# Sums of h stored in the v stage, two gate/up splits moved, and another product order in a block's first step

## The chip, the cores and the metric

One core of a Trainium2 chip runs one program. TensorE (PE) multiplies, VectorE (DVE), ScalarE (ACT) and GpSimd (POOL) work element by element, and SyncE (SP) issues nearly all the DMAs. The metric is the device time of one execution in microseconds, and the figure is the median of several runs.

## The reference

One layer of a flow-matching backbone runs on 128 context tokens and 512 latent tokens with a model width of 2048. Everything is float32.

```python
sh1, sc1, g1, sh2, sc2, g2 = adaln(cond, w_ada, b_ada)        # silu(cond) @ w_ada, split in 6
h = rms_norm(x, norm1_g) * (1 + sc1) + sh1
q, k, v, u = split(h @ w_in, 4)                               # 2048 x 4096; q and k normed per head
attn = neighbourhood_attention(q, k, v, cache_k, cache_v, rpb)  # context tokens: dense attention
pool = (centred window means of u, minus u) @ w_pool * pool_scale
x = x + g1 * (concat(rms_norm(attn), rms_norm(pool)) @ w_out)
h = rms_norm(x, norm2_g) * (1 + sc2) + sh2
x = x + g2 * ((silu(h @ w_gate) * (h @ w_up)) @ w_down)       # width 5632
```

The outputs are x for both kinds of tokens and the keys and values of the context tokens.

## The kernel before

All 640 tokens are one operand. Activations lie transposed: a tile has 128 features in the partitions and 640 tokens in the free dimension.

**The large products.** Every float32 operand is split in a high and a low float32r part (hi and lo), and a product takes three matmuls: hi by hi, lo by hi, hi by lo (L400, L401, L402 in `products`). On top of that each pair of weight tiles by a pair of activation tiles goes through a seven-product scheme. A *step* is one pair of 128-row weight tiles: seven products, 21 matmuls of 128x320 or 128x322. A *block* is the steps that add up in the same seven PSUM banks (eight steps in the input, output, gate and up stages, four or five in the down stage). At the end of a block `combine` reads the banks: ACT copies the first (L408), and seven sums on DVE follow (L407). The third and the fourth sum after it read the bank of product 3 and, for the second time, that of product 2.

**Work around a step.** `fetch` loads a weight pair four steps ahead (tile wf, three buffers), `sums` forms the weight sums three steps ahead on POOL (L327), `x_hi` and `x_lo` split them two steps ahead on ACT (L336) and DVE (L342). Other work is hung on later steps with `at`.

**The v stage** comes first. For each of 8 pairs of feature tiles (a *v block*), `turn` transposes the normed x, ACT and DVE write the modulated h (hhi by L244, the float32 h in two reused tiles c by L245), and POOL forms hlo (L246). Then 10 groups of six 128x512 matmuls give v (L163 to L165), added up by DVE (L682). SP loads w_in for it (raw, L148) and, during the first half, the shift and scale part of w_ada (araw, L196, three buffers); the transposes and the adaLN products for the next v blocks are in between.

**The first input block** needs sums of h for the seven-product scheme. `plan_h` puts hi and lo together again into tile f (L628), forms the three sums (`y_sum`, L361), and splits them into h's own tile and t (ACT L636, L637; DVE or POOL L644). A planner (`issue`) writes this order out from durations and due times, together with the first eight steps, and it picks DVE or POOL for each operation.

**The gate and up stage** has 22 pairs of blocks, a gate block and an up block. After the up block of a pair, its end work hangs on the next steps by the tables FF_TIGHT, FF_WIDE and FF_LAST, in half steps: scale by rho (L1654), add the shift (L1659), multiply by the gate (L1642), sums (L1669), and four splits (`f_split`, ACT L1679 and DVE L1680) that are stored to DRAM (L1683, L1684). FF_WIDE holds for pairs 4 to 20. The down stage loads these operands back (L1703).

The instructions of every engine stand in the order that the program writes from the first input block on; in the v stage PE's order is written, and a scheduler sets that of the others.

Of the kernel before, what the change touches and what calls it, by code (L numbers as in the profile page):

```python
# [9 lines left out]
F32 = mybir.dt.float32  # L10
# [8 lines left out]
P = 128  # L19
# [30 lines left out]
def tile_hybrid_step(  # L50
# [51 lines left out]
    def c_tile(i):  # L102
        return cp.tile([P, 2 * HX], F32, tag=f"c{i}", name=f"c{i}", bufs=1)
# [9 lines left out]
    c_s = dram.tile([P, NKT, 32], F32, name="c_s")  # L113
    x_s = dram.tile([NKT, P, TOK], F32, name="x_s")
    h2_s = dram.tile([NKT, P, TOK], F32, name="h2_s")

    yh_s = dram.tile([NPAIR, P, 7, HB], F32, name="yh_s")
    yl_s = dram.tile([NPAIR, P, 7, HB], F32, name="yl_s")
# [107 lines left out]
    def turn(kt, eng=nc.gpsimd):  # L226


        by_column = lambda v: v.rearrange("p (c r) -> p c r", r=ROWS)
        ps_s = pp.tile([P, 512], F32, tag="tp", name="ps_s")  # L230
        ps_p = pp.tile([P, P], F32, tag="tq", name="ps_p")
        for t in range(4):
            nc.tensor.transpose(ps_s[:, t * P : (t + 1) * P], xn[t][:, kt * P : (kt + 1) * P], ident)
        nc.tensor.transpose(ps_p, xn[4][:, kt * P : (kt + 1) * P], ident)
        h = c_tile(kt % 2)[:, 0:TOK]
        hi, lo = h_hi[kt], h_lo[kt]
        for s in range(2):
            g, b = gs[1][:, kt, s : s + 1], sh[1][:, kt, s : s + 1]
            if s == 0:
                src = ps_s.rearrange("p (r c) -> p c r", r=ROWS)  # L240
                to = [by_column(v[:, 0:SMP]) for v in (hi, h)]
            else:
                src, to = ps_p, [v[:, SMP:TOK] for v in (hi, h)]
            nc.scalar.activation(to[0], src, AF.Identity, bias=b, scale=g)  # L244
            nc.vector.tensor_scalar(to[1], src, g, b, op0=ALU.mult, op1=ALU.add)  # L245
        eng.tensor_tensor(lo, h, hi.bitcast(F32), op=ALU.subtract)  # L246

    starts = [(k, 2) for k in range(0, NKT, 2)]
    done = [0]
# [37 lines left out]


    PRODUCTS = ((6, 6), (1, 1), (0, 0), (2, 2), (3, 5), (5, 3), (4, 4))
    EARLY_FIRST = (0, 4, 6, 1, 2, 3, 5)  # L290
    GROUPS = ((0, 4), (4, 9), (9, 13), (13, 18), (18, 22))
    YB = 7
# [104 lines left out]
    def products(ps, x, y, first, last, order):  # L397
        for n in order:
            b, (i, j) = ps[n], PRODUCTS[n]
            mm(b, lhsT=x[0][:, i, :], rhs=y[j][0], start=first, stop=False)  # L400
            mm(b, lhsT=x[0][:, i, :], rhs=y[j][1], start=False, stop=False)  # L401
            mm(b, lhsT=x[1][:, i, :], rhs=y[j][0], start=False, stop=last)  # L402
# [11 lines left out]
        add(c[2], c[2], p4)  # L414
        add(c[0], c[0], p2)

    def step(ps, y, first, out, order=range(7), last=False):

        s = now[0]
        now[0] = s + 1  # L420
        fetch(s + 4)
        sums(s + 3)
        if out is None:
            prepare(s + 2)
        for fn, args in jobs.pop((s, 0), ()):
            fn(*args)
        products(ps, xs.pop(s), y, first, last or out is not None, order)
        if out is not None:
            combine(ps, out)
            prepare(s + 2)  # L430
        for fn, args in jobs.pop((s, 1), ()):
            fn(*args)
# [186 lines left out]
    t_tiles = {}  # L619

    def plan_h(i, key):
        g, s = place("f"), place("f")
        y = lambda: (four(s, HB), four(g, HB))

        def join(e, j):
            d = g.tile[:, 2 * j * HB : 2 * j * HB + TOK]
            kt = 2 * i + j
            E[e].tensor_tensor(d, h_hi[kt].bitcast(F32), h_lo[kt].bitcast(F32), op=ALU.add)  # L628

        got = take(key, g, s)  # L630
        joined = [on("DVE Pool", key, TOK, lambda e, j=j: join(e, j), (got,), (g,)) for j in range(2)]
        summed = plan_y_sums(key, y, g, s, HB, joined)

        def hi(e):
            t_tiles[i] = [tl.tile([P, 3, HB], F32R, name=f"t{n}{i}") for n in ("hi", "lo")]
            nc.scalar.copy(h_hi[2 * i + 1][:, HB:TOK], four(s, HB)[:, 0, :])  # L636
            nc.scalar.copy(t_tiles[i][0], four(s, HB)[:, 1:4, :])  # L637

        def lo(e, part):
            if part == 0:  # L640
                out, src, minus = h_lo[2 * i + 1][:, HB:TOK], four(s, HB)[:, 0, :], h_hi[2 * i + 1][:, HB:TOK]
            else:
                out, src, minus = t_tiles[i][1], four(s, HB)[:, 1:4, :], t_tiles[i][0]
            E[e].tensor_tensor(out, src, minus.bitcast(F32), op=ALU.subtract)  # L644

        his = on("ACT", key, 4 * HB, hi, summed, (s,))
        return [
            on("DVE Pool", key, n, lambda e, part=part: lo(e, part), (his,), (s,)) for part, n in ((0, HB), (1, 3 * HB))
        ]

    def h_operand(i):
        out = []
        for h, t in zip((h_hi, h_lo), t_tiles[i]):
            even, odd = h[2 * i], h[2 * i + 1]
            out.append([odd[:, HB:TOK], t[:, 0, :], t[:, 1, :], t[:, 2, :], even[:, 0:HB], even[:, HB:TOK], odd[:, 0:HB]])
        return list(zip(*out))


# [2 lines left out]
    for b, (k0, n) in enumerate(starts):  # L661
        more = b + 1 < len(starts)
        if not more:
            close(sp_cm)
            gu = ctx.enter_context(tc.tile_pool(name="gu", bufs=1, side="right", reuse_waits="tile"))
            fp_cm, fp = pool("fp", side="right")
            for s in range(3):
                fetch(s)
        group = 0
        for vb in range(2):  # L670
            raw = load_k(w_in, k0, n, 2 * AW + vb * 512, 512, wp.tile([P, 1024], F32, tag="raw", name="raw", bufs=3)[:, 0 : n * 512])
            ws = [split(raw[:, i * 512 : i * 512 + 512]) for i in range(n)]
            for t in range(NT):
                tk = slice(t * P, (t + 1) * P)
                ps = pp.tile([P, 512], F32, tag="g", name="g", bufs=4)
                for i in range(n):
                    mm3(ps, h_hi[k0 + i][:, tk], h_lo[k0 + i][:, tk], *ws[i], i == 0, i == n - 1)
                dst = vacc[t][vb]
                if b == 0:
                    nc.scalar.copy(dst, ps)  # L680
                else:
                    nc.vector.tensor_tensor(dst, ps, dst, op=ALU.add)  # L682
                next(stream, None)
                if more and group == 5:
                    ada_until(b + 2)
                if more and 5 <= group < 5 + starts[b + 1][1]:
                    turn(starts[b + 1][0] + group - 5)
                group += 1
            if not more:
                store_v(vb)  # L690
# [1024 lines left out]
    ada_gen = None  # L1715

    FF_TIGHT = (0, 1, 2, 4, 6, 7, 18, 20)
    FF_WIDE = (2, 4, 6, 8, 10, 12, 18, 20)
    FF_LAST = (2, 3, 4, 8, 16, 18, 10, 12)
    WIDE = 4  # L1720

# [258 lines left out]
```

## Time and profile before

| | |
|---|---|
| three runs | 2805.04, 2805.74, 2812.82 us; median 2805.74 us |
| profiled execution | 2810.24 us, span 2808.4 us, mean granted clock 0.972 |
| busy share of the span | PE 93%, POOL 70%, DVE 67%, ACT 39% |
| v stage | from the start to 206.05 us |
| input blocks | 206.05 us to about 585 us, the first of them to 263.07 us |
| gate and up stage | about 1032 us to 2209.5 us |

PE's ends are modelled and its matmuls overlap, so its busy share says little about its pace; the pace is read from the starts of the matmuls and from the number of them in a stretch. A step is 21 matmuls. Windows are named by their first and last microsecond from the start of the span.

### The profile page before, as it was taken

What the parts mean: (1) busy time and instruction counts of PE and PEld (TensorE: products, weight loads), DVE (VectorE), ACT (ScalarE), POOL (GpSimd) and SP (SyncE); (2) the same over time, 40 slices, a digit from 0 to 9 for tenths busy, and PEclk for the clock granted to TensorE, in tenths of its full rate; (3) what the DMA queues carried; (4) which work ended last, traced back from release to release, by engine and by line L of the source; (5) the groups of instructions that cost most, each with busy time, mean ns of one, the idle gap of its engine ahead of it and who ended that gap; (6) DMA issues with size and microseconds to landing.
All of it is one profiled execution on the core that took longest, in us unless ns stands there. A gap on an engine that the chain in (4) does not pass through costs nothing.

```text
span 2808.4 us, 46345 instructions
## 1 busy us (share of the span) xinstructions
PE 2622.1 (93%) x16936; PEld 2429.6 (87%) x16936; DVE 1891.1 (67%) x2566; ACT 1088.7 (39%) x1605; POOL 1968.2 (70%) x2264
## 2 busy tenths in 40 slices
PE   5997999988769968998999999999999899999998
PEld 2577888877669968998999999999999889999997
DVE  2478433457875597665787776777867667787776
ACT  3233222246633434443444444444444323333333
POOL 2367565667678876675788877887778656887874
PEclk9998999989989988999999999999999999999999
DMA  9922777677335443655344343343443775365353
GB/s 324 322 88 68 258 261 269 236 211 220 95 123 194 156 146 124 218 169 160 116 135 130 116 142 123 122 142 117 135 130 116 264 242 202 122 220 191 114 166 104
DMA packets 367222, 476.69 MB, mean 170 GB/s; under 512 B 22544, under 2 KB 286224, under 8 KB 366352
## 3 DMA queue, kind: packets, MB, share of 16 engines
q1 hardware_dynamic: 363824, 468.87, 51.2%
q10 hardware_dynamic: 3168, 4.85, 0.6%
q8 instruction: 133, 2.18, 0.3%
q14 instruction: 97, 0.79, 0.1%
HBM read 389.09 MB, written 84.54 MB: 169 GB/s over the span
## 4 chain that ended last, share of the span: by engine, by line
PE 34%; DVE 11%; POOL 7%; DMA 7%; issue 4%; ACT 3%; SPq 0%; ACTq 0%; DVEq 0%; POOLq 0%
PE pp L402 11%; PE pp L400 11%; PE pp L401 11%; POOL wf L327 6%; DVE xlo L342 3%; DVE c L407 2%; ACT xhi L336 2%; DMA wf<-in_w_up_dram 2%; DMA wf<-in_w_gate_dram 2%; DMA wf<-in_w_down_dram 2%; DMA ylo<-yl_s 1%; DVE cx L407 1%; DVE c L1680 1%; DMA araw<-in_w_ada_dram 1%; DVE cx L1680 0%
## 5 line engine op out<-in xcount | busy, mean ns | idle before, releaser
L327 POOL TENSOR_TENSOR wf<-wf 128x128 f32<-128x128 f32 (+1 forms) x2007 | 1642.7, 825 | 574.1 <-DMA wf<-in_w_up_dram 112.9
L400 PE MATMUL pp<-yhi,xhi 128*128 128x322 f32 (+1 forms) x4072 | 1282.9, 315 | 29.5 <-DVE c L407 8.9
L402 PE MATMUL pp<-yhi,xlo 128*128 128x322 f32 (+1 forms) x4072 | 1278.3, 314 | 17.1 <-DVE xlo L342 13.9
L401 PE MATMUL pp<-ylo,xhi 128*128 128x322 f32 (+1 forms) x4072 | 1269.6, 312 | 18.5 <-DVE ylo L381 8.4
L342 DVE TENSOR_TENSOR xlo<-wf,xhi 128x896 fp32r<-128x896 f32 x678 | 809.4, 1202 | 667.9 <-ACT xhi L336 648.6
L336 ACT CAST xhi<-wf 128x896 fp32r<-128x896 f32 x688 | 648.1, 943 | 1241.3 <-POOL wf L327 1091.5
L400 PEld LDWEIGHTS pp<-yhi,xhi 128*128 128x128 f32 x4072 | 775.5, 190 | 60.9 <-DVE c L407 15.4
L402 PEld LDWEIGHTS pp<-yhi,xlo 128*128 128x128 f32 x4072 | 775.2, 190 | 30.6 <-DVE xlo L342 25.8
L401 PEld LDWEIGHTS pp<-ylo,xhi 128*128 128x128 f32 x4072 | 775.5, 190 | 20.7 <-DVE ylo L381 9.3
L407 DVE TENSOR_TENSOR c<-c,pp 128x320 f32<-128x320 f32 (+1 forms) x581 | 253.9, 484 | 44.9 <-ACT c L408 29.2
L400 PE MATMUL pp<-hhi,xhi 128*128 128x320 f32 x384 | 124.7, 325 | 3.1 <-DVE v L682 3.1
L402 PE MATMUL pp<-hhi,xlo 128*128 128x320 f32 x384 | 121.1, 315 | 0.4 <-DVE xlo L342 0.4
L401 PE MATMUL pp<-hlo,xhi 128*128 128x320 f32 x384 | 121.1, 315 | 0.0
L401 PE MATMUL pp<-tlo,xhi 128*128 128x320 f32 x288 | 92.5, 321 | 16.5 <-DVE tlo L644 16.5
L159 POOL TENSOR_TENSOR wlo<-raw,whi 128x512 fp32r<-128x512 f32 x32 | 41.9, 1330 | 81.7 <-ACT whi L158 79.9
L400 PEld LDWEIGHTS pp<-hhi,xhi 128*128 128x128 f32 x384 | 74.0, 193 | 21.9 <-issue 15.1
L402 PE MATMUL pp<-thi,xlo 128*128 128x320 f32 x288 | 91.5, 318 | 0.0
L400 PE MATMUL pp<-thi,xhi 128*128 128x320 f32 x288 | 91.4, 317 | 0.1
L682 DVE TENSOR_TENSOR v<-g,v 128x512 f32<-128x512 f32 x70 | 48.0, 688 | 47.5 <-PE g L165 47.5
L402 PEld LDWEIGHTS pp<-hhi,xlo 128*128 128x128 f32 x384 | 74.0, 193 | 0.7 <-DVE xlo L342 0.7
L401 PEld LDWEIGHTS pp<-hlo,xhi 128*128 128x128 f32 x384 | 74.2, 193 | 0.0
L401 PEld LDWEIGHTS pp<-tlo,xhi 128*128 128x128 f32 x288 | 56.0, 194 | 18.6 <-DVE tlo L644 18.6
(248 smaller groups left out, 2663.4 us busy)
## 6 DMA issues: line engine op xcount, KB each, us to landing
araw<-in_w_ada_dram SPq DMA_DIRECT2D x60, 1024.0 KB, 6.8
wf<-in_w_gate_dram SPq DMA_DIRECT2D x176, 256.0 KB, 2.8
wf<-in_w_up_dram SPq DMA_DIRECT2D x176, 256.0 KB, 3.0
wf<-in_w_down_dram SPq DMA_DIRECT2D x176, 256.0 KB, 3.0
araw<-in_w_ada_dram SPq DMA_DIRECT2D x64, 512.0 KB, 6.6
wf<-in_w_in_dram SPq DMA_DIRECT2D x96, 256.0 KB, 4.1
yh_s<-yh SPq DMA_DIRECT2D x66, 320.0 KB, 3.7
wf<-in_w_out_dram SPq DMA_DIRECT2D x64, 256.0 KB, 2.7
```

The lines of the kernel that those rows point to most:

```text
L159: nc.gpsimd.tensor_tensor(lo, raw, hi.bitcast(F32), op=ALU.subtract)
L327: tt = lambda o, a, b, op: eng.tensor_tensor(o, a, b, op=op)
L336: nc.scalar.copy(hi, raws[s][:, 0:7, :])
L342: eng.tensor_tensor(lo, f[:, 0:7, :], hi.bitcast(F32), op=ALU.subtract)
L400: mm(b, lhsT=x[0][:, i, :], rhs=y[j][0], start=first, stop=False)
L401: mm(b, lhsT=x[0][:, i, :], rhs=y[j][1], start=False, stop=False)
L402: mm(b, lhsT=x[1][:, i, :], rhs=y[j][0], start=False, stop=last)
L407: add = lambda o, a, b: nc.vector.tensor_tensor(o, a, b, op=ALU.add)
L682: nc.vector.tensor_tensor(dst, ps, dst, op=ALU.add)
L1680: nc.vector.tensor_tensor(v, v, hi.bitcast(F32), op=ALU.subtract)
```

## The change

Three edits, and the lines of the file move down by up to 15.

1. In each v block DVE overwrites the two float32 tiles of h with the sums that the scheme needs (`t_sums`, four subtractions of 128x320), and SP stores both tiles to a new DRAM tensor t_s (`t_store`, two DMAs of 320 KB). `plan_h` no longer joins and sums: one DMA of 640 KB loads the four quarters into f. The order of the sums within f differs, and `h_operand` follows it.
2. A block's first step runs its products in the order 0, 1, 3, 2, 4, 5, 6 (FREE_FIRST).
3. FF_WIDE moves the second split of the sums from half step 12 to 22, and the two splits of the product from 18 and 20 to 24 and 26. The entries are in the order scale, shift, times, sums, split of sums 0 and 1, split of the product 0 and 1; here the sums' first split stays at 10.

```diff
+    t_s = dram.tile([NKP, P, 2, TOK], F32, name="t_s")
...
+    h_now = [None, None]
+    def t_sums():
+        (y21, y22), (y11, y12) = ((v[:, 0:HB], v[:, HB:TOK]) for v in h_now)
+        for o, a, b in ((y11, y12, y11), (y12, y22, y12), (y22, y22, y11), (y21, y21, y22)):
+            nc.vector.tensor_tensor(o, a, b, op=ALU.subtract)
+    def t_store(i):
+        for q in range(2):
+            nc.sync.dma_start(t_s[i][:, 1 - q, :], h_now[q])
...
+    FREE_FIRST = (0, 1, 3, 2, 4, 5, 6)
...
-        products(ps, xs.pop(s), y, first, last or out is not None, order)
+        products(ps, xs.pop(s), y, first, last or out is not None, order or (FREE_FIRST if first else range(7)))
...
     def plan_h(i, key):
-        g, s = place("f"), place("f")
-        y = lambda: (four(s, HB), four(g, HB))
-        def join(e, j):
-            d = g.tile[:, 2 * j * HB : 2 * j * HB + TOK]
-            kt = 2 * i + j
-            E[e].tensor_tensor(d, h_hi[kt].bitcast(F32), h_lo[kt].bitcast(F32), op=ALU.add)
-        got = take(key, g, s)
-        joined = [on("DVE Pool", key, TOK, lambda e, j=j: join(e, j), (got,), (g,)) for j in range(2)]
-        summed = plan_y_sums(key, y, g, s, HB, joined)
+        s = place("f")
+        got = op("none", 0.0, key - 6, lambda: None, taken, (s,))
+        taken[:] = [got]
+        loaded = dma(key - 6, 655, lambda: [(s.tile[:, 0 : 4 * HB], t_s[i].rearrange("p a n -> p (a n)"))], (got,), (s,))
+        summed = [loaded]
...
+                if group == 1:
+                    t_sums()
+                if group == 3:
+                    t_store(b)
...
-    FF_WIDE = (2, 4, 6, 8, 10, 12, 18, 20)
+    FF_WIDE = (2, 4, 6, 8, 10, 22, 24, 26)
```

**SP in the v stage.** Before, from the last loads of w_ada (araw) on:

```order
L196 DMA araw<-in_w_ada_dram 128x4x256 x8
L148 DMA raw<-in_w_in_dram 128x2x512
L196 DMA araw<-in_w_ada_dram 128x4x256 x6
L148 DMA raw<-in_w_in_dram 128x2x512 x9
L321 DMA wf<-in_w_in_dram 128x2x256 x3
```

The same place now, c_826 and c_854 being the two tiles of h of v block 3:

```order
L197 DMA araw<-in_w_ada_dram 128x4x256 x6
L260 DMA t_s<-c_612 128x640
L260 DMA t_s<-c_640 128x640
L197 DMA araw<-in_w_ada_dram 128x4x256 x2
L149 DMA raw<-in_w_in_dram 128x2x512
L197 DMA araw<-in_w_ada_dram 128x4x256 x8
L149 DMA raw<-in_w_in_dram 128x2x512
L197 DMA araw<-in_w_ada_dram 128x4x256 x6
L260 DMA t_s<-c_826 128x640
L260 DMA t_s<-c_854 128x640
L149 DMA raw<-in_w_in_dram 128x2x512 x5
```

The stores of v blocks 0, 1 and 2 stand in front of loads of w_ada; those of block 3 and later do not. At the end of the v stage the loads of f stand so, v_155 being the last tile of v:

```order
L293 DMA v_s<-v_153 128x512
L293 DMA v_s<-v_155 128x512
L294 DMA out_dram<-v_155 128x512
L528 DMA f_1624<-t_s 128x1280
L528 DMA f_1625<-t_s 128x1280
L528 DMA f_1626<-t_s 128x1280
L336 DMA wf<-in_w_in_dram 128x2x256
```

The load for the first step (f_1616) is issued four stores earlier in the same queue; those for the later steps stand behind the last store of v.

**DVE in the first input block.** Before, a stretch in its middle:

```order
L628 TENSOR_TENSOR f_1770<-hhi_119,hlo_135 128x640
L628 TENSOR_TENSOR f_1770<-hhi_120,hlo_136 128x640
L644 TENSOR_TENSOR hlo_132<-f_1708,hhi_116 128x320
L644 TENSOR_TENSOR tlo_1746<-f_1708,thi_1745 128x960
L342 TENSOR_TENSOR xlo<-wf,xhi 128x896
L361 TENSOR_TENSOR f_1789<-f_1770 128x2x320
L628 TENSOR_TENSOR f_1821<-hhi_121,hlo_137 128x640
L361 TENSOR_TENSOR f_1789<-f_1770,f_1789 128x320
```

Now, the same place (here L653 is the split, L342 a weight sum and L357 xlo):

```order
L653 TENSOR_TENSOR hlo_129<-f_1625,hhi_113 128x320
L342 TENSOR_TENSOR wf<-wf 128x128 x2
L342 TENSOR_TENSOR wf<-wf 128x256
L653 TENSOR_TENSOR tlo_1700<-f_1626,thi_1699 128x960
L653 TENSOR_TENSOR hlo_133<-f_1660,hhi_117 128x320
L357 TENSOR_TENSOR xlo<-wf,xhi 128x896
```

The joins and the sums of f are gone, and only splits, weight sums and xlo are left; POOL's rows lose the same two kinds.

**DVE in the gate and up stage**, at the end of a gate block. Before, with cx_12756 and cx_12757 the sums of the pair before and c the gate's result:

```order
L342 TENSOR_TENSOR xlo<-wf,xhi 128x896
L1680 TENSOR_TENSOR cx_12756<-cx_12756,yh 128x2x320
L342 TENSOR_TENSOR xlo<-wf,xhi 128x896
L1680 TENSOR_TENSOR cx_12757<-cx_12757,yh 128x2x320
L407 TENSOR_TENSOR c_13313<-c_13312,pp 128x322
```

The same place now:

```order
L357 TENSOR_TENSOR xlo<-wf,xhi 128x896
L1693 TENSOR_TENSOR cx_12762<-cx_12762,yh 128x2x320
L357 TENSOR_TENSOR xlo<-wf,xhi 128x896
L422 TENSOR_TENSOR c_13319<-c_13318,pp 128x322
L422 TENSOR_TENSOR c_13318<-c_13319,pp 128x322
```

The second split no longer stands between the last xlo and the first sum of `combine`; it and the other two now follow the scaling by rho of the gate's result, one a step.

## Rows read from the trace of the kernel before

**Rows 1.** Windows: us; busy of PE, PEld, DVE, ACT, POOL; PEclk; DMA; GB/s.

```profile
69.17:123.72 54.55, 52.17 (x289) 27.50 (x285) 23.05 (x43) 11.69 (x21) 17.48 (x14) 1.00 1.06 344
145.00:190.00 45.00, 44.18 (x207) 35.81 (x206) 26.79 (x43) 13.41 (x24) 24.41 (x19) 1.00 0.20 64
...
206.05:263.07 57.02, 36.84 (x170) 33.94 (x169) 56.61 (x52) 16.45 (x22) 46.02 (x35) 0.77 0.18 59
263.07:288.16 25.09, 25.09 (x169) 25.09 (x169) 11.60 (x15) 7.89 (x9) 11.48 (x18) 0.98 0.58 190
```

**Rows 2.** Group of DVE, 145 to 190 us: busy, mean ns, idle before.

```profile
L682 DVE TENSOR_TENSOR v<-g,v 128x512 f32<-128x512 f32 x30 | 20.7, 689 | 14.6 <-PE g L165 14.6
```

**Rows 3.** Wait of PE, 190 to 263.1 us: total, times, longest.

```profile
PE pp L401 <- DVE tlo L644: 16.5, 7, 3.9
```

**Rows 4.** Groups of DVE in the first input block.

```profile
L628 DVE TENSOR_TENSOR f<-hhi,hlo 128x640 f32<-128x640 f32 x8 | 9.9, 1254 | 0.0
...
L361 DVE TENSOR_TENSOR f<-f,f 128x320 f32<-128x320 f32 x4 | 5.4, 1359 | 0.0
...
L361 DVE TENSOR_TENSOR f<-f 128x640 f32<-128x640 f32 x3 | 3.1, 1043 | 0.0
```

**Rows 5.** Groups of POOL in the same stretch.

```profile
L361 POOL TENSOR_TENSOR f<-f,f 128x320 f32<-128x320 f32 x10 | 13.8, 1380 | 5.9 <-DVE f L361 5.7
...
L628 POOL TENSOR_TENSOR f<-hhi,hlo 128x640 f32<-128x640 f32 x4 | 8.1, 2013 | 1.1 <-DVE tlo L644 1.1
L361 POOL TENSOR_TENSOR f<-f 128x640 f32<-128x640 f32 x4 | 8.0, 2002 | 2.1 <-DVE tlo L644 1.6 <-DVE f L361 0.5
```

**Rows 6.** Timeline of DVE in the first input block: start, duration.

```profile
211.68 1.15 DVE L644 TENSOR_TENSOR tlo<-f,thi 128x960 fp32r<-128x960 f32 x1
...
225.72 2.50 DVE L644 TENSOR_TENSOR tlo<-f,thi 128x960 fp32r<-128x960 f32 x1
...
230.99 0.48 DVE L361 TENSOR_TENSOR f<-f,f 128x320 f32<-128x320 f32 x1
```

**Rows 7.** DMA issues: count, KB each, median us from issue to landing.

```profile
araw<-in_w_ada_dram SPq DMA_DIRECT2D x33, 512.0 KB, 6.6
...
yh_s<-yh SPq DMA_DIRECT2D x66, 320.0 KB, 3.7
```

**Rows 8.** Timeline of SP's DMA issues at the v stage's end.

```profile
210.20 0.48 SPq L280 DMA_DIRECT2D out_dram<-v  x1
```

**Rows 9.** Windows of the gate and up stage.

```profile
1593.58:1618.45 24.87, 24.87 (x170) 24.87 (x169) 19.69 (x22) 10.49 (x18) 20.38 (x23) 1.00 0.32 92
1618.45:1644.78 26.33, 25.65 (x170) 24.91 (x169) 18.18 (x24) 12.07 (x18) 21.40 (x27) 1.00 0.53 167
1340.15:2209.50 869.35, 860.28 (x5714) 846.13 (x5712) 640.64 (x745) 381.92 (x577) 690.08 (x811) 1.00 0.43 134
1365.04:1371.60 6.56, 6.56 (x44) 6.12 (x43) 6.46 (x10) 2.52 (x3) 3.48 (x5) 1.00 0.56 186
...
2181.62:2189.20 7.58, 7.05 (x43) 6.17 (x43) 7.38 (x12) 2.52 (x3) 4.04 (x6) 1.00 0.65 210
```

**Rows 10.** Timeline of DVE at the end of gate block 7.

```profile
1463.53 1.35 DVE L342 TENSOR_TENSOR xlo<-wf,xhi 128x896 fp32r<-128x896 f32 x1
1464.80 1.35 DVE L1680 TENSOR_TENSOR c<-c,yh 128x640 f32<-128x640 f32 x1
1466.08 3.20 DVE L407 TENSOR_TENSOR cx<-cx,pp 128x322 f32<-128x322 f32 x7
```

**Rows 11.** Timeline of PE in the first step of up block 7.

```profile
1466.61 0.41 PE L400 MATMUL pp<-yhi,xhi 128*128 128x322 f32 x1 [0.30 <-DVE cx L407]
...
1467.60 0.41 PE L400 MATMUL pp<-yhi,xhi 128*128 128x322 f32 x1 [0.28 <-DVE cx L407]
```

**Rows 12.** Timeline of DVE there: the fourth sum of `combine`.

```profile
1467.58 0.49 DVE L407 TENSOR_TENSOR cx<-cx,pp 128x322 f32<-128x322 f32 x1
```

**Rows 13.** Window from the last up block into the down stage.

```profile
2188.00:2224.00 36.00, 31.69 (x200) 29.32 (x198) 18.98 (x22) 13.61 (x24) 23.27 (x30) 0.99 0.96 349
```

More of the change, by code (lines that the diff above doesn't have):

```diff
@@ L235, in turn @@
         h = c_tile(kt % 2)[:, 0:TOK]
+        h_now[kt % 2] = h
         hi, lo = h_hi[kt], h_lo[kt]
@@ L415, in combine, with step @@
         add(c[0], c[0], p2)
-    def step(ps, y, first, out, order=range(7), last=False):
+    def step(ps, y, first, out, order=None, last=False):
         s = now[0]
@@ L654, in h_operand @@
             even, odd = h[2 * i], h[2 * i + 1]
-            out.append([odd[:, HB:TOK], t[:, 0, :], t[:, 1, :], t[:, 2, :], even[:, 0:HB], even[:, HB:TOK], odd[:, 0:HB]])
+            out.append([odd[:, HB:TOK], t[:, 2, :], t[:, 0, :], t[:, 1, :], even[:, 0:HB], even[:, HB:TOK], odd[:, 0:HB]])
         return list(zip(*out))
```

## The prediction

> **What bounds the kernel now.** I read the windows by stage first, then PE's waits in the stage that stands out, then the groups and timelines of the engines that it waits for. The profiled execution took 2810.24 us; the median of the runs is 2805.74 us, 4.5 us lower, so I make the sum against 2810.24 and take the difference off the median.
>
> Nearly everywhere PE sets the pace: an input block takes 25.09 us for its eight steps when nothing disturbs it [rows 1], a gate block 24.87 us [rows 9], 3.11 us a step and 0.148 us a matmul. Three places are slower. (a) In the first half of the v stage DMA is full: 1.06 of its time at 344 GB/s over 54.55 us, while PE is busy 52.17 us and DVE 23.05 [rows 1]; that is two v blocks, 27.3 us each. In the second half DMA idles (0.20), PE is full, and DVE has 18 of 45 us free; 30 additions of v are in them, ten a block, so a block takes 15 us and a group 1.5 us [rows 1, 2]. (b) The first input block takes 57.02 us for eight steps. DVE is busy 56.61 us of them and POOL 46.02; PE waits 16.5 us for tlo, seven times, and the granted clock is 0.77 there against 0.98 in the next block [rows 1, 3]. So DVE with POOL bounds it. (c) The 17 gate and 17 up blocks of pairs 5 to 21 take 869.35 us; 34 blocks of 24.87 would be 845.6, so 23.8 us are lost [rows 9]. I took the first two steps of each of the 17 up blocks as a window: first and last are 6.56 and 7.58 us [rows 9], together they are 122.8 us, where a quarter of a quiet block is 6.22 and 17 of them 105.7. So 17.1 of the 23.8 us lie there. Rows 10 and 11 show why: on DVE an xlo, a split, and only then, at 1466.08, the first sum of `combine`; PE's second product starts at 1466.61, its third at 1467.60, each behind a sum that frees its bank.
>
> **Part 1, the first input block.** Removed on DVE: 9.9 + 5.4 + 3.1 = 18.4 us of joins and sums [rows 4]; on POOL 13.8 + 8.1 + 8.0 = 29.9 [rows 5]. Of 56.61 + 46.02 = 102.6 us of work 54.3 are left, 27.2 on each engine if shared evenly, a little over PE's own 25.09. To it comes a start: the load for the first step is early, but the next three stand behind the last store of v, issued at 210.20 to 210.68 [rows 8], 4.6 us into the block; a 320 KB store lands after 3.7 us and a 512 KB load in a full queue after 6.6 [rows 7], so the second operand of 640 KB is there 8 to 11 us into the block, and its ACT and DVE split after that, while the first step keeps PE only 3 us. Half of that gap is caught up while the engines work ahead: 4 us. I take 27.2 + 4 = 31.2 us, 25.8 saved. Bounds: not under 25.09 (32 saved), not over 57.02 (nothing saved).
>
> **Part 1, the v stage.** Added: 32 subtractions of 128x320 on DVE and 16 stores of 320 KB. In the second half a subtraction of 0.48 us [rows 6], four a block, 1.9 us, goes into 18 free of 45 us, nearly three blocks: nothing. In front of them in DVE's queue is the wait for POOL's hlo, and behind them are the additions of v; those have four PSUM banks to wait in, so PE does not see 1 or 2 us. In the first half the cover is gone, since DMA is full. The stores of v blocks 0, 1 and 2 stand in front of loads of w_ada: 3 x 0.655 MB = 1.97 MB, at 344 GB/s 5.7 us [rows 1]. Those of block 3 come behind the last such load. SP waits at a store until the subtractions are done, and the loads of w_ada behind it wait too; in block 0 the transposes come right before, in blocks 1 and 2 half a block earlier, so I count no wait. I take +5.7. Bounds: 0 if PE, which idles only 2.4 of 54.55 us [rows 1], is what bounds the stage after all; +11.5 if SP waits the length of a block's four subtractions, 1.9 us, in front of the loads in each of three blocks.
>
> A store must land before the next `turn` writes the same tile. The sums are done with the end of the transposes' work, half a v block before the next transposes: 7.5 us in the second half, 13 us in the first [rows 1, 2]. Landing takes 3.7 to 6.6 us [rows 7]. So it fits, by 3 us or more in the second half, where DMA is idle and 3.7 us hold.
>
> **Shared ports.** A split of 128x960 on DVE took 1.15 us beside an idle POOL and 2.50 us beside a POOL sum [rows 6]. The Trainium skill (SBUF — State Buffer, Who interferes with whom) says that a DVE instruction with two SBUF inputs and a GpSimd instruction that reads SBUF lock each other out for the whole instruction; the two rows agree. The subtractions are such instructions, in a stage where PE waits for POOL's splits of w_in, so the rule speaks against this part. With the rows' price the worst is 32 x 0.48 = 15.4 us. I count nothing, because POOL is busy 24.41 of 45 and 17.48 of 54.55 us there [rows 1], and keep 15.4 as a rival.
>
> **Part 2, the order of a first step.** The third product already starts at 1467.60, when the fourth sum, which reads product 2 for the last time, has run for 0.02 us [rows 11, 12]. So before the change the third product writes the bank that the third sum frees; the pool hands out banks as they come free. With product 3 in third place it will get the same bank at the same time: 0, in all stages. Bounds: if the banks were fixed it would be worth the length of a sum, 3.20/7 = 0.46 us [rows 10], in the 17 up blocks, 7.8 us either way.
>
> **Part 3, the splits.** The second split stands between xlo and the first sum and takes 1.28 us to the next start [rows 10]. Without it the sums start at 1464.80, and PE's second product, due at about 1466.15, 0.46 us earlier than it started [rows 11], finds its bank free. Over the 17 up blocks a head start of 1.28 us leaves 1.5 of the 17.1 us. The moved splits fall in steps 4 to 6 of the up block, where DVE has little but an xlo of at most 1.35 us in 3.11 us and each split adds at most 1.35; a slip of 1.1 us in total is allowed: 17.1 − 1.5 − 1.1 = 14.5 saved. Bounds: 17.1, and 0 if the wait only moves. ACT's casts and SP's stores move with them; SP waits for the split behind a weight load that is due a step later anyway. For pair 20 they move into the stretch where the down operands are loaded: DMA is 0.96 busy there at 349 GB/s [rows 13]. 0.655 MB of stores more are in it, 1.9 us. The other 6.7 us of (c) stay.
>
> **The sum.** −25.8 + 5.7 − 14.5 + 1.9 = −32.7: 2810.24 − 32.7 = 2777.5 for the profiled execution, 2805.74 − 32.7 = 2773.0 for the median.
>
> **Rivals.**
> - The first block gets a new bound: the loads of f come one after another behind the stores of v, or four buffers of f are too few, and it takes 45 us. For it: issue to landing is 3.7 to 6.6 us, longer than a step. Against it: DMA is 0.18 busy there [rows 1]. 13.8 us less: 2787.
> - The late splits only move the wait to the next `combine` or a late xlo: 14.5 less, 2787.5. For it: DVE is busy 18.18 of 26.33 us even in an up block [rows 9]. Against it: those steps have idle DVE time.
> - Everything is hidden: stores cost 0, the first block takes 27 us, the splits give 17.1 and the down loads cost 0: 2805.74 − 30 − 17.1 = 2758.6.
> - Slower: the stores hold up `turn`. In-place sums keep the two tiles of h until both stores have landed, and SP issues the second behind a weight load that waits for its own buffer. If it lands after the transposes, DVE stops with ten additions of v behind it, and PE stops when its four banks are full. It decides from 3 + 6 us later than I reckon (four groups of 1.5 us). At 6 us in each of 7 blocks it is +42: 2815. Against it: the margin above.
> - The port lock hits PE each time: +15.4, 2788.
>
> **Chances.** Forecast 0.63, late loads 0.13, moved wait 0.10, all hidden 0.07, lock 0.03, slower 0.04. The likeliest case by itself reaches from 2764 to 2783. The range 2758 to 2792 takes in the two rivals at 2787 and the lock, and the edge of the case in which all is hidden. About 0.3%, 8.4 us, is what a measurement can tell from no change. All cases but the slower one end at 2788 or below, so faster 0.93; same 0.03, for mishaps that add up; slower 0.04.
>
> **What would show it.** The first input block in 29 to 34 us with DVE no longer full and a clock near 1; the DMA-full part of the v stage 5 to 6 us longer, with no wait of DVE for a store; the third product of an up block behind the third sum, as now; the first two steps of up blocks at 6.2 to 6.5 us; the first down steps some 2 us later against their block. It is wrong if the first block stays over 40 us, if up blocks still lose over 0.5 us each, or if v blocks after the loads of w_ada take over 16 us.

## The result, and the profile after

The changed kernel took 2795.64 us (median of 7 runs, 2789.57 to 2800.82); the kernel before, run beside it, 2812.82 us (7 runs). The ratio is 0.9944, 95% interval [0.9931, 0.9956]: faster by some 16 us, half of the 32.7 us forecast, and the time lies 3.6 us above the range. The forecast was added to the 2805.74 us of the first three runs; the median of the seven beside the changed kernel is 7.1 us higher, so the ratio and the stages say more about the miss than the distance to the range. The profiled execution took 2795.32 us against 2810.24 before, 14.9 us less.

The starts of the matmuls divide the two profiled executions into the same stretches (us, from the first matmul of one to that of the next):

| stretch | before | after | forecast | measured |
|---|---|---|---|---|
| v stage, from the span's start | 206.1 | 209.1 | +5.7 | +3.0 |
| first input block | 57.0 | 39.2 | −25.8 | −17.8 |
| second input block | 25.1 | 27.3 | 0 | +2.2 |
| other input blocks | 293.4 | 293.5 | 0 | 0 |
| attention, with the last input step | 198.0 | 194.3 | 0 | −3.7 |
| output blocks | 252.4 | 254.8 | 0 | +2.4 |
| gate and up, pairs 0 to 4 | 308.2 | 308.0 | 0 | −0.2 |
| gate and up, pairs 5 to 21 | 869.4 | 866.1 | −14.5 | −3.3 |
| down stage, first group | 122.4 | 123.6 | +1.9 | +1.2 |
| down stage, the rest, to the last matmul | 465.0 | 465.9 | 0 | +0.9 |
| sum | | | −32.7 | −15.3 |

Two rows carry the miss: pairs 5 to 21 by 11.2 us, and the first two input blocks by 10.2. Windows of the kernel after, with the columns of [rows 1]; they are the DMA-full half of the v stage (two v blocks), its second half, the first and the second input block, pairs 5 to 21, and the stretch of [rows 13] in its new place:

```profile
69.30:128.20 58.90, 54.12 (x288) 27.89 (x285) 23.86 (x47) 11.72 (x21) 19.00 (x14) 0.97 1.05 343
150.00:195.00 45.00, 44.36 (x209) 36.05 (x208) 34.82 (x54) 13.68 (x24) 25.46 (x20) 1.00 0.31 109
209.11:248.28 39.17, 30.48 (x169) 28.56 (x167) 26.72 (x28) 17.04 (x24) 20.03 (x16) 0.87 0.64 228
248.28:275.57 27.29, 25.37 (x170) 24.76 (x169) 15.63 (x23) 7.86 (x9) 13.21 (x21) 1.00 0.58 195
1326.10:2192.15 866.05, 858.55 (x5714) 847.17 (x5712) 645.97 (x745) 381.65 (x577) 720.56 (x811) 1.00 0.43 133
2173.00:2209.00 36.00, 30.07 (x183) 28.31 (x181) 19.66 (x24) 14.81 (x25) 24.20 (x29) 0.95 0.99 362
```

The DMA-full half is 58.90 us long where it was 54.55 [rows 1], at the same 343 GB/s: more bytes. The second half still has PE full, although DVE is busy 34.82 of 45 us, 8 us more. In the first input block DVE and POOL are no longer full (26.72 and 20.03 us; 56.61 and 46.02 before), and yet it takes 39 us: something else bounds it. In pairs 5 to 21 POOL is busy 720.56 us with the same 811 instructions that took 690.08 [rows 9].

**What the first input block waits for.** PE's waits, 195 to 256 us, total, times and longest:

```profile
PE pp L415 <- DVE v L691: 4.4, 1, 4.4
PE pp L416 <- DVE tlo L653: 2.1, 2, 1.3
PE pp L415 <- DVE c L422: 1.9, 2, 1.6
```

The seven waits for tlo, 16.5 us [rows 3], are down to two, and the longest is new: an addition of v. The timelines of ACT, DVE and SP say why (start, duration, and in brackets the idle time before and what ended it):

```profile
211.89 0.46 ACT L645 CAST hhi<-f 128x320 fp32r<-128x320 f32 x1 [8.52 <-DMA f<-t_s]
```

```profile
212.38 0.49 DVE L653 TENSOR_TENSOR hlo<-f,hhi 128x320 fp32r<-128x320 f32 x1 [3.39 <-ACT hhi L645]
212.78 1.28 DVE L691 TENSOR_TENSOR v<-g,v 128x512 f32<-128x512 f32 x2
```

```profile
204.99 0.43 SPq L528 DMA_DIRECT2D f<-t_s  x1
...
207.68 6.74 SPq L293 DMA_DIRECT2D v_s<-v  x5
214.47 0.45 SPq L294 DMA_DIRECT2D out_dram<-v  x1
214.97 1.61 SPq L528 DMA_DIRECT2D f<-t_s  x3
```

The load of f issued at 204.99 landed at 211.86. DVE's split hlo needs it, and stands in DVE's queue in front of the last two additions of v. So those waited 3.4 us, PE waited 4.4 us for the banks that they free, SP waited with the last stores of v, and behind these the loads of f for steps 2 to 4 went out only at 214.97.

**What the up blocks do now.** The first and last windows of [rows 9], the first two steps of an up block, were 6.56 and 7.58 us; the windows in the same two blocks after:

```profile
1351.00:1357.25 6.25, 6.25 (x44) 6.25 (x43) 4.11 (x7) 1.89 (x2) 4.97 (x6) 1.00 0.39 115
2165.00:2171.70 6.70, 6.70 (x44) 6.27 (x43) 4.85 (x8) 1.49 (x2) 4.95 (x6) 1.00 0.47 146
```

So what was aimed at was hit: of the 17.1 us lost there, 4.0 are left. But the last steps of the 17 gate blocks lose 8.1 us where they lost 2.4, and the first two steps of gate blocks 4.7 where they lost 0.4. PE's waits in pairs 5 to 21 after are these two:

```profile
PE pp L417 <- DVE xlo L357: 4.9, 12, 1.1
PE pp L415 <- DVE cx L422: 0.6, 2, 0.3
```

PE now waits for weights (xlo), and hardly for the sums. The list holds 5.5 us of the 18.5 that these 34 blocks lose against a quiet block (one that nothing disturbs, 24.93 us); the rest shows only in the starts of the matmuls. The view that explains it is ACT's waits, 1400 to 2100 us, of the kernel before and then after (total, times, longest):

```profile
ACT xhi L336 <- POOL wf L327: 332.3, 178, 4.4
ACT c L408 <- PE pp L402: 13.5, 13, 2.0
ACT xhi L336 <- PE pp L401: 10.7, 5, 2.1
```

```profile
ACT xhi L351 <- POOL wf L342: 347.2, 181, 4.3
ACT xhi L351 <- PE pp L416: 12.1, 4, 4.0
```

The cast xhi writes one of three buffers, the last readers of which are matmuls. If the weights were ahead of PE, it would wait for PE. It waits mostly for POOL's sums instead, in both kernels. POOL's sums wait for the load, and the load for a free buffer, as SP's waits in the kernel before say:

```profile
SPq L321 <- DVE xlo L342: 516.1, 210, 5.0
```

The ring is closed: load, sums, cast, xlo, and again the load of three steps later. Over pairs 6 to 20 the issue of nearly every load ends 0.4 us after the end of the xlo that frees its buffer (means by step 0.39 to 0.54 us before and 0.40 to 0.49 after, worked out from the 240 loads). While that is so, no load can make up lateness, whatever engine is idle.

### The profile page after: what moved, and what is told of

Same layout as the page of the kernel before. It is cut to its first block, busy times and chain, and to the rows that moved or that the text cites. A ratio compares the mean times of both kernels' runs of the same rounds, so it can differ in the third digit from the quotient of the medians.

```text
span 2793.1 us, 46356 instructions
## 1 busy us (share of the span) xinstructions
PE 2616.0 (94%) x16936; PEld 2424.4 (87%) x16936; DVE 1882.4 (67%) x2578; ACT 1087.4 (39%) x1605; POOL 1970.8 (71%) x2244
## 4 chain that ended last, share of the span: by engine, by line
PE 61%; DVE 15%; DMA 9%; POOL 7%; issue 4%; ACT 3%; SPq 1%; ACTq 0%; DVEq 0%; POOLq 0%
PE pp L417 18%; PE pp L415 18%; PE pp L416 17%; POOL wf L342 5%; DVE xlo L357 3%; DMA wf<-in_w_down_dram 2%; DVE c L422 2%; PE x L758 2%; ACT xhi L351 1%; DMA raw<-in_w_in_dram 1%; DMA araw<-in_w_ada_dram 1%; DMA wf<-in_w_out_dram 1%; DMA wf<-in_w_gate_dram 1%; DVE wf L342 1%; DMA wf<-in_w_up_dram 1%
## 5 line engine op out<-in xcount | busy, mean ns | idle before, releaser
L342 POOL TENSOR_TENSOR wf<-wf 128x128 f32<-128x128 f32 (+1 forms) x2004 | 1669.2, 840 | 558.0 <-DMA wf<-in_w_down_dram 110.5
L415 PE MATMUL pp<-yhi,xhi 128*128 128x322 f32 (+1 forms) x4072 | 1282.7, 315 | 25.8 <-ACT c L423 7.1
L357 DVE TENSOR_TENSOR xlo<-wf,xhi 128x896 fp32r<-128x896 f32 x678 | 799.0, 1186 | 662.0 <-ACT xhi L351 650.2
L165 PE MATMUL g<-wlo,hhi 128*128 128x512 f32 x160 | 64.8, 405 | 5.5 <-POOL wlo L160 5.3
```

The lines of the kernel that those rows point to most:

```text
L165: mm(out, lhsT=xhi, rhs=wlo, start=False, stop=False)
L342: tt = lambda o, a, b, op: eng.tensor_tensor(o, a, b, op=op)
L357: eng.tensor_tensor(lo, f[:, 0:7, :], hi.bitcast(F32), op=ALU.subtract)
```

## The experiments

All kernels start from the changed one unless said otherwise; ratios are to the kernel before. Single profiled executions give the windows.

**1. The old places of the splits.**

```diff
-    FF_WIDE = (2, 4, 6, 8, 10, 22, 24, 26)
+    FF_WIDE = (2, 4, 6, 8, 10, 12, 18, 20)
```

> The changed kernel with the old places of the gate and up splits (half steps 12, 18, 20). Theory A, weights loop: a weight tile's way (load, sums on POOL, cast on ACT, xlo on DVE, and back to the load that waits for the buffer) runs without slack in the gate and up stage, so the moved splits only changed where PE waits: pairs 5 to 21 come back from 866 to about 869 us and the time rises by about 3 us, to 2799. Theory B, the prediction's own term: the splits are worth 14.5 us, and something else of the changed kernel took 11 us away: 2807 to 2810, with about 877 us for pairs 5 to 21.

Ratio 0.9960 [0.9947, 0.9972], 2802 us: the moved splits are worth about 4.5 us by the ratios, whose intervals overlap, and 5.2 by pairs 5 to 21:

```profile
1328.31:2199.54 871.23, 861.71 (x5714) 847.03 (x5712) 636.85 (x745) 381.20 (x577) 697.78 (x811) 1.00 0.44 133
```

Against theory B (14.5 us, 877 in this stretch), for A (869). The first two steps of up blocks lose 17.1 us again.

**2. A fourth weight buffer, in pairs 4 to 21.** There was room for one of seven slots; the third weight sum is written over its own operand, so that seven do.

```diff
-            raws[s] = f = gu.tile([P, 8, P], F32, tag="wf", name="wf", bufs=3)
+            more = wfx is not None and s % 4 == 3
+            raws[s] = f = (
+                wfx.tile([P, 7, P], F32, tag="wfx", name="wf", bufs=1)
+                if more
+                else gu.tile([P, 7, P], F32, tag="wf", name="wf", bufs=3)
+            )
...
```

> The changed kernel with a fourth buffer for the weight pairs from pair 4 of the gate and up stage to its end (each buffer has seven slots in place of eight, one sum being written over its own operand). Theory A, weights loop: the load no longer waits for the xlo of three steps before, so the lateness of one step is gone by the next block's end; gate blocks no longer lose 0.5 to 1.4 us in their last step, pairs 5 to 21 take 848 to 853 us in place of 866, and the time falls by 13 to 18 us, to about 2780. Theory C, DVE's queue: the last step waits because the xlo stands behind the sums and the split on DVE whatever comes before; then a buffer more gives under 3 us.

Ratio 0.9871 [0.9854, 0.9889], 2777 us, 20 us below the changed kernel. Pairs 5 to 21:

```profile
1322.41:2169.92 847.51, 847.51 (x5715) 847.51 (x5714) 669.43 (x750) 381.91 (x578) 695.31 (x808) 1.00 0.45 136
```

That is 34 blocks of 24.93 us with PE busy all the time, and in 1400 to 2100 us no wait of PE is listed. ACT's waits have turned round: the cast now waits for PE as well, 184 us of it, and less for POOL.

```profile
ACT xhi L357 <- PE pp L422: 119.6, 55, 2.2
ACT xhi L357 <- POOL wf L348: 104.3, 64, 3.1
ACT xhi L357 <- PE pp L423: 64.5, 50, 2.1
```

The whole loss of pairs 5 to 21 was lateness of the weights. Theory C falls: xlo still stands behind the same work on DVE. The experiment changes two things, the number of buffers and the seven slots. From the up block of pair 0 to that of pair 3 there are three buffers with either layout, and five of these seven blocks take the same time to 0.01 us with seven slots as with eight, while the other two vary with either; so the layout by itself shows no gain there. Seven slots with three buffers in pairs 5 to 21 were not run.

**3. Four buffers and the old places of the splits.** Experiment 1's line on top of experiment 2.

> The changed kernel with the fourth weight buffer from pair 4 on and with the old places of the splits. Theory A, weights loop: the xlo and the split that stand in front of the first sum of combine were late only because the weights were; with a buffer more they run earlier, and pairs 5 to 21 take 850 to 855 us (847.5 with the new places and four buffers, 871.2 with the old places and three). Theory H, order on DVE: the split in front of the sums costs its 1.1 us a pair however early the weights are; then the 17 us in the first two steps of up blocks stay, and pairs 5 to 21 take 862 to 866 us.

Ratio 0.9872 [0.9856, 0.9889], 2777.5 us; pairs 5 to 21:

```profile
1327.94:2175.45 847.51, 847.51 (x5714) 847.51 (x5713) 657.08 (x745) 382.58 (x577) 687.61 (x808) 1.00 0.45 137
```

The same 847.51 us to the last digit. With weights in time the place of the splits is worth nothing, though the second split stands in front of the sums as before the change. Theory H, which is the prediction's reading, falls; A holds further than expected (850 to 855).

**4. Four buffers in the kernel before**, nothing else of the change.

> The kernel before with the fourth weight buffer from pair 4 on and nothing else. Theory A, weights loop: the 23.8 us that pairs 5 to 21 lose are all lateness of the weights, so they take 34 blocks of 24.88, 845.9 us in place of 869.4, and the ratio to the kernel before is 0.991 to 0.992, more than the whole change gave. If the prediction's reading were right (the second split in front of the sums), 17 us of it would stay, and the ratio would be 0.998.

Ratio 0.9911 [0.9895, 0.9928], 2787 us: one weight buffer gives more than the three edits together. Pairs 5 to 21 take 34 blocks of 24.88:

```profile
1337.44:2183.36 845.92, 845.92 (x5715) 845.92 (x5714) 659.11 (x746) 382.55 (x577) 691.88 (x809) 1.00 0.45 137
```

**5. The old order of a first step.**

```diff
-        products(..., order or (FREE_FIRST if first else range(7)))
+        products(..., order or range(7))
```

> The changed kernel with a block's first step in the old order of products. The prediction counted this edit at 0: no change beyond 0.1%, 2794 to 2797. Theory F: the order itself costs 0.04 us in every quiet first step of the gate and up stage (3.14 against 3.10 us), so without it pairs 5 to 21 are about 1.4 us shorter. Theory G: the order saves the length of a sum, 0.46 us, at each of the 17 up blocks, then 7.8 us slower, 2803.

Ratio 0.9936 [0.9922, 0.9949]: no change that the time can tell, so theory G falls. The profile tells more. A quiet block, the gate block of pair 5, after and in this kernel:

```profile
1326.10:1351.00 24.90, 24.90 (x170) 24.90 (x169) 20.63 (x26) 10.70 (x16) 19.12 (x23) 1.00 0.34 103
```

```profile
1326.43:1351.31 24.88, 24.88 (x171) 24.88 (x169) 20.27 (x25) 10.69 (x16) 19.09 (x23) 1.00 0.35 100
```

The first window is cut short: from matmul to matmul that block takes 24.93 us after and 24.88 here, in every quiet block alike; what in the order costs it, the profile does not show. It is why 847.51 (experiments 2 and 3) and 845.92 (experiment 4) differ by 1.6 us. So the edit costs 0.047 us a block, and theory F holds.

**6. Early loads of f.** In the last v block the loads for the first four steps go out one after each of the first groups.

```diff
+                if not more and group < 4:
+                    f_early(group)
...
-        loaded = dma(key - 6, 655, lambda: [(s.tile[:, 0 : 4 * HB], t_s[i].rearrange("p a n -> p (a n)"))], (got,), (s,))
+        loaded = got if i < 4 else dma(key - 6, 655, lambda: [(s.tile[:, 0 : 4 * HB], t_s[i].rearrange("p a n -> p (a n)"))], (got,), (s,))
```

> The changed kernel with the loads of f for the first four steps of the first input block issued from the start of the last v block, ahead of the last stores of v. Theory D: the first block takes 39 us because the split of f stands on DVE in front of the last two additions of v and waits for a load of 6.9 us, and the loads of the next steps stand behind the stores of v that wait for those additions; then the block takes 27 to 30 us, the next one 25 to 27, and the time falls by 10 to 12 us to about 2785. Theory E: the splits themselves on ACT, DVE and POOL set its pace; then the block stays at 34 us or more and the time falls by 5 us or less.

Ratio 0.9908 [0.9894, 0.9923], 2787.5 us. The first two input blocks:

```profile
210.14:243.02 32.88, 27.02 (x170) 26.22 (x168) 29.51 (x31) 14.93 (x20) 19.10 (x18) 0.95 0.57 188
243.02:268.76 25.74, 25.26 (x171) 24.66 (x169) 13.92 (x20) 7.86 (x9) 14.76 (x22) 1.00 0.61 199
```

6.3 and 1.6 us less, so theory D holds for most of the loss, but 32.9 is not its 27 to 30. (The v stage in front of them ended 1.0 us later, at 210.1 us, and at 209.8 to 213.5 in experiments 7, 8 and 10, which have the same loads.) What is late next: the third step alone takes 9.2 us and waits 4.3 us for an xlo on POOL,

```profile
PE pp L417 <- POOL xlo L357: 4.3, 1, 4.3
```

and on POOL that xlo stands behind the sums of the fourth step's weights:

```profile
216.45 1.86 POOL L342 TENSOR_TENSOR wf<-wf 128x128 f32<-128x128 f32 x3 [13.15 <-DVE tlo L657]
218.28 1.68 POOL L657 TENSOR_TENSOR hlo<-f,hhi 128x320 fp32r<-128x320 f32 x2
219.92 2.91 POOL L357 TENSOR_TENSOR xlo<-wf,xhi 128x896 fp32r<-128x896 f32 x1
```

```profile
212.06 0.38 SPq L336 DMA_DIRECT2D wf<-in_w_in_dram  x1
```

POOL had been idle for 13 us when those sums came, 4.0 us after the end of the issue of their load. That load stands behind the last stores of v, and it went out 0.02 us after the first step's xlo, which frees its buffer and stands on DVE behind the last additions of v; the late xlo itself had had its cast since 213.4 us.

**7. Both: a fourth weight buffer and early loads.**

> The fourth weight buffer from pair 4 on together with the early loads of f. The two gains lie in different stages, so they add: 20 us and 8 to 10 us off the changed kernel, 2764 to 2769, ratio 0.983 to 0.985. If the earlier end of the input stage were given back later, it would stay at 2775.

Ratio 0.9855 [0.9842, 0.9869], 2769.9 us. Just above the expected ratios; the early loads gave about 4.5 us on top by the ratios, though the second input block ended 6.0 us earlier by the profile than in experiment 2. The intervals of the two ratios overlap, so what is missing can't be told from noise.

**8. The fourth weight buffer in the first input block too.**

```diff
+            wfx = fp
-            for s in range(3):
+            for s in range(4):
                 fetch(s)
...
```

> As the run before the last but with a fourth weight buffer in the first input block too, so that the fourth weight load no longer waits for the xlo of the first step, which stands behind the last additions of v. With early loads of f alone the first block took 32.9 us, 9.2 of it in the third step, which waited for an xlo. Theory I: that weight load is what was late; then the third step takes 3 to 5 us, the block 27 to 29 us, and the time falls by another 4 us, to about 2762. Theory J: DVE and POOL are what is full; then the block stays above 31 us and the time is that of the run with both edits.

Ratio 0.9853 [0.9837, 0.9868]: the time of experiment 7. The third step fell from 10.7 us there to 3.1, as theory I said, but the sixth rose from 3.4 to 6.9 and the block took 32.0 us. Neither theory is right as it stood: the load was late, and behind it DVE is nearly full.

```profile
210.49:242.50 32.01, 27.29 (x169) 26.23 (x168) 30.70 (x33) 15.12 (x20) 15.80 (x14) 0.95 0.56 187
```

DVE is busy 30.70 of 32.01 us and POOL only 15.80, and PE's longest waits in the block are for an xlo on DVE:

```profile
PE pp L423 <- DVE xlo L363: 3.4, 2, 1.9
```

So what the planner gives to DVE and what to POOL is next to try; that was not run.

**9. Fewer stores in the v stage.**

```diff
-                if group == 3:
+                if group == 3 and b > 2:
                     t_store(b)
...
-        loaded = dma(key - 6, 655, lambda: [(s.tile[:, 0 : 4 * HB], t_s[i].rearrange("p a n -> p (a n)"))], (got,), (s,))
+        loaded = dma(key - 6, 655, lambda: [(s.tile[:, 0 : 4 * HB], t_s[max(i, 3)].rearrange("p a n -> p (a n)"))], (got,), (s,))
```

> The changed kernel without the stores of the sums of v blocks 0, 1 and 2 (the first input block loads the sums of v block 3 in their place, so the output is not the reference's). The prediction: 1.97 MB fewer in the part of the v stage where DMA is full, so the v stage ends 4.9 to 5.7 us earlier, with the first matmul of the input stage at about 204 in place of 209 us and the time about 5 us lower. Rival: the v stage is longer because the four subtractions a block delay the additions of v on DVE or SP's order delays the loads; then taking the stores away gives under 2 us.

Ratio 0.9933 [0.9921, 0.9946], some 3 us below the changed kernel, with overlapping intervals. The first input matmul comes at 204.83 us, against 207.2 to 209.4 in the changed kernel and the other four that load f at its time and store all sums. The same two v blocks as in the first window above take 56.80 us:

```profile
68.30:125.10 56.80, 52.58 (x289) 27.55 (x285) 25.03 (x48) 11.72 (x21) 17.96 (x14) 1.00 1.03 333
```

The fifth v block starts at 145.4 us, 3.8 earlier than in the changed kernel, of the 4.8 us that the change had added there; in the other four it starts at 147.7 to 150.0. So by the trace the stores are most of that cost, and the rival falls; the time alone would not show it, and the 4.9 to 5.7 us expected were not quite reached.

**10. Fourth buffer, early loads and the old order of products.**

> Fourth weight buffer from pair 4 on, early loads of f, and a block's first step in the old order of products. With the buffers no longer late the order has no wait to save, and a quiet block with it was 0.047 us longer: pairs 5 to 21 take 845.9 us in place of 847.5. The whole is about 2 us below the run with both edits, 2767 to 2769, which the time alone can hardly tell from it; if the order were still needed, blocks would be over 25 us.

Ratio 0.9855 [0.9834, 0.9877], 2770.8 us: with experiments 7 and 8 the fastest version, and the three can't be told apart; the 2767 to 2769 us expected were just missed, inside the noise. Pairs 5 to 21 are at the expected 845.92 us:

```profile
1324.74:2170.66 845.92, 845.92 (x5715) 845.92 (x5714) 666.93 (x748) 381.63 (x577) 694.65 (x810) 1.00 0.44 136
```

## Why the prediction was wrong

**The splits (−14.5 forecast, −3.3 measured).** The place itself came out nearly as forecast: of the 17.1 us in the first two steps of the up blocks 1.5 were to stay, and 4.0 did, 13.1 saved. The step that failed is "a slip of 1.1 us in total is allowed": 9.8 us came back on balance, in the gate blocks above all (5.7 in their last steps, 4.3 in their first two). Behind it stands the reading "Without it the sums start at 1464.80", which took DVE's queue at that place, an xlo, a split, the sums [rows 10], for the cause. But the xlo in it ran when its weights came. Experiments 3 and 4 leave the split where it was, and the 17 us are gone. The loss belonged to the ring of weight buffers; it showed at the sums because DVE's work there was late together with the xlo. With the splits moved the weights came later against PE: xlo ended on average 2.5 us ahead of the fourth up step before and 1.4 after, 1.9 and 1.0 ahead of the first gate step, and at the last gate step it ended after that step had begun, by 0.6 us on average (means over pairs 6 to 20). PE's stops in the up blocks had given the weights time to catch up, and the moved splits lie beside POOL's sums (last section); how much each of the two did was not run. That "those steps have idle DVE time" was true and no argument: in a closed ring an engine's idle time is the time in which its input is on the way. The forecast named the rival "the late splits only move the wait" at 0.10; experiments 2 and 3 show that it was right, and why. The size of −3.3 is not firm: experiments 6 and 9 run the same instructions in this stretch as the changed kernel and took 862.82 and 862.90 us there, 3.2 us less than its 866.07, so against experiment 1, which differs in the places of the splits alone, moving them is worth 5.2 to 8.4 us. It is not worth 14.5.

**The signs of being wrong.** None of the three that the prediction named came: the first block took 39.2 us and not over 40, the up blocks lose 0.4 us each (1.2 before) and not over 0.5, and the late v blocks took 15.2 us and not over 16. They watched the places that were to gain. The gate blocks, where the time went (0.8 us each, 0.2 before), had no sign.

**The first input block (−25.8 forecast; −17.8, and +2.2 in the next).** The engines' work fell as reckoned: DVE and POOL were busy 46.8 us together, under the 54.3 reckoned, though some of it moved into the second block (28.8 us there, 23.1 before). Two steps failed. One is "the load for the first step is early". It went out 4.1 us ahead of the first matmul and took 6.9 us, and its split was written in front of two additions of v. That "the next three stand behind the last store of v" was seen; that this store itself would wait for that split was not. The other is "Half of that gap is caught up while the engines work ahead". The second operand landed 11.5 us into the block, near the 8 to 11 reckoned, and nothing was caught up: the first two steps took 17.3 us and the other six 21.9, where a quiet block's are 6.2 and 18.5. The term of 4 us for the late start should have been about 12. The mean granted clock in the block was 0.87 (0.77 before) and not near 1 as forecast. Experiment 6 takes the wait away and gets 7.8 us of the 10.2 back. This is the rival "late loads", 45 us at 0.13, at about three fifths of its size.

**Two rivals at once.** Both came true in part. They were priced as alternatives at 2787 each; nothing kept them from adding, and together at full size they are 2801. That case was missing, and with it the upper end of the range.

**What held, and what did not.** The stores: +5.7 forecast, 4.8 at the start of the fifth v block, 3.8 of which experiment 9 takes away with them; the table's +3.0 is less because the last v block took 14.3 us where it took 15.9. That SP would not wait at a store held for v blocks 1 and 2 and was wrong for block 0: of the 37.3 us that SP waited for the subtractions, in 8 places, 8.3 lie there, in front of loads of w_ada, and the others in blocks 4 to 7, behind these loads. The second v block still started at 69.3 us (69.2 before), so the wait in block 0 shows no cost by then; experiment 9 takes it away together with the bytes, so the two are not told apart. DVE shows no wait for a store in the v stage, so no `turn` waited for one, and v blocks after the loads of w_ada took 15.2 us. The subtractions cost PE nothing there, although each took 0.49 or 1.13 us and not 0.48:

```profile
L256 DVE TENSOR_TENSOR c<-c,c 128x320 f32<-128x320 f32 x6 | 6.8, 1133 | 0.0
L256 DVE TENSOR_TENSOR c<-c 128x320 f32<-128x320 f32 x5 | 2.5, 492 | 2.3 <-POOL hlo L248 2.2
```

A block of v has 15 us; its four subtractions, 3.1 us of DVE's time in place of the 1.9 reckoned, went into DVE's free time. The order of the first step: 0 was right for the time, and the measured size is +0.047 us a block, 1.6 us in pairs 5 to 21. The down loads: +1.9 forecast, +1.2 in the table; but experiment 1, which does not move the stores, took 124.1 us in that stretch where the changed kernel took 123.6, so this term is not shown.

## What to carry to other kernels

Before a wait at one place is priced, ask whether the engines that feed it are ever ahead: if the cast that refills a buffer waits for its input and never for the consumer, and the load waits for the buffer each time, then the ring sets the pace, a cure at one place only moves the wait, and a buffer more is what to try first; here it gave all of it back. Put a sign of being wrong at the places that are to lose nothing, too. An instruction that waits for a DMA must not be queued in front of one that frees a bank or feeds a store: look at what stands behind it on its engine, and at what stands behind that on the queue of the stores. Rivals that don't exclude each other are priced together too.

## What the runs showed of the hardware that was not expected

The same 811 instructions of POOL in pairs 5 to 21 took 690.08 us in the kernel before and 697.78 in experiment 1, with the splits in the old places and three buffers; 713.82 to 720.56 us in the four profiles with the new places and three buffers; and 695.31 in experiment 2, with the new places and four buffers. What changed is what DVE does beside them. In the changed kernel's trace a weight sum of 128x128 took 0.45 to 0.47 us in all 216 cases where DVE was idle or only read PSUM with one of its two inputs, and 0.97 us on average, up to 1.39, in the 272 where DVE ran only instructions with two SBUF inputs beside it; in the kernel before these were 253 and 219. One of each, with DVE's instruction beside it:

```profile
1602.76 0.46 POOL L342 TENSOR_TENSOR wf<-wf 128x128 f32<-128x128 f32 x1 [0.41 <-DVE c L422]
1602.67 0.48 DVE L422 TENSOR_TENSOR c<-c,pp 128x322 f32<-128x322 f32 x1
```

```profile
1611.95 1.04 POOL L342 TENSOR_TENSOR wf<-wf 128x128 f32<-128x128 f32 x1
1611.31 1.35 DVE L1667 TENSOR_TENSOR c<-c,rho 128x640 f32<-128x640 f32 x1
```

The Trainium skill (SBUF — State Buffer, Who interferes with whom) says that a DVE instruction with two SBUF inputs and a GpSimd instruction that reads SBUF exclude each other; the splits and the weight sums are such a pair, and the numbers agree with it. How much of these 16 to 30 us reached PE was not run.

The attention stage, which none of the edits touches, took 193.86 us in experiment 2's profile and 201.48 in experiment 8's, with a mean granted clock of 0.93 and 0.86 (1 is the upper of the two levels, 2.4 GHz, and 0.5 the lower, 1.2 GHz):

```profile
569.36:763.22 193.86, 157.49 (x994) 130.43 (x992) 146.99 (x332) 113.65 (x235) 128.74 (x130) 0.93 0.63 186
```

```profile
561.06:762.54 201.48, 168.53 (x993) 140.46 (x991) 147.77 (x332) 113.98 (x235) 127.41 (x130) 0.86 0.61 179
```

So the −3.7 us of that stage in the table of the result can't be put down to the change, nor the +2.4 us of the output blocks, which took 251.9 to 255.1 us in the twelve profiles: a stage of a single profile is no measure for differences of a few microseconds there. Pairs 5 to 21 repeated to 0.01 us where the weights were in time (847.50 or 847.51 us in four profiles), but not with three buffers: 866.07, 862.82 and 862.90 us with the same instructions.
